# A two-layer S5 and gMLP trunk: the factors of B sent through DRAM on SyncE's queue, C's turn behind the first rows, both halves of two tables loaded at once, and the last sums of the scan on VectorE

## The chip, the core and the metric

One core of a Trainium2 chip runs the whole kernel. The metric is the device time of one execution in microseconds. Three runs of the kernel before gave 986.35, 982.47 and 985.27, a median of 985.27.

## The reference, cut

Two layers, each a stack of three post-normalised sub-layers on 256 tokens of width 1024: a SwiGLU feed-forward of width 2816, a mixer, and a second feed-forward. The mixer of the first layer is an S5 state-space model, that of the second a gMLP gate. The change touches the S5 mixer and its preparation alone:

```python
u = x @ w_in                                              # 256 x 1024, in 64 groups of 16 channels
lam = exp(a * dt)                                         # complex, 64 groups x 64 states
coef = (lam - 1) / a                                      # complex
bbar = coef[..., None] * b                                # complex, (group, state, channel)
bu = einsum('blgc,gpc->lbgp', u_groups, bbar)
h[t] = lam * h[t - 1] + bu[t]                             # scan over 256 tokens
y = Re(einsum('lbgp,gcp->blgc', h, c)) + d * u
y = gelu(y)
z = y * sigmoid(y @ w_glu + b_glu)
out = z @ w_out
```

## The kernel before, in words

Every product runs on TensorE in float32r with weights and activations split in two parts, `hi` and `lo`, and three matmuls for each product (`mm3`, `mm3t`). The weights are a single stream of blocks of 128 x 2048 (class `Stream`): SyncE loads a block into one of three `raw` buffers (line 63), ScalarE rounds it to `hi` (line 88 or 115), VectorE subtracts to get `lo` (line 89 or 119), and five pairs of split buffers are there. A load waits until the `lo` of the block that had its buffer is done, so SyncE's queue stands in the order of the program between loads and everything else that it issues. `tick` is called after every group of matmuls: it finishes the `lo` of the block before, issues the next load, rounds the next block, and calls one piece of background work.

The first feed-forward works through 11 chunks of 256 columns: four groups of 24 matmuls for the way in (lines 208 to 210, tile `ips`) and two groups of 12 for the way out of the chunk two before (lines 201 to 203, tile `acc`), six ticks in all.

Beside it runs the preparation of S5 (`prepare_s5`), as that background work: a list of steps, each with a first tick and a cost in us; a tick has 1.5 us of credit, and steps are taken from the list in order while credit is left. Steps of cost 0 are on other engines than VectorE. The ones that matter here:

- `coefs` and `coef` (lines 749 to 764): the discretisation factors of B, four complex sets, on VectorE.
- `spread` (769): writes these factors to DRAM and reads them back in another layout, 32 partitions at a time, five DMAs on GpSimd's queue. `load_b` and `c_load` (32 and 16 DMAs) and `seed` (small products for the tables) are on GpSimd too. The reads wait for the write to have landed.
- `c_turn` (905): VectorE transposes C, which `c_load` has brought; `b_rows` (844) multiplies B with the factors read back, and `b_turn` (853) transposes the result and sends it to DRAM as `rows`. `b_rows` and `b_turn` come eight times, `c_turn` ahead of the first.
- `table` (808) and `c_lam` (914): rotation tables and C times powers of lambda, both written to the DRAM tensor `tc`, half 0 and half 1 of its columns.

The mixer itself (`s5`) turns the scan over 256 tokens into eight tiles `ct` of 128 channels. For each: `inject` (TensorE, 16 matmuls `pps`), `forward` (a rotation on VectorE, `turned`, then two sums on GpSimd), `scan` (VectorE), `back` (rotation on VectorE, then two `sums` on GpSimd, into the one buffer `h`), `read_out` (TensorE, `yps`, which reads `h` and both halves of the table), `activate` (VectorE line 1118, then GELU on ScalarE), `split_y` (GpSimd), and `gate` (TensorE, `gacc`). The loop in lines 1225 to 1264 skews these over the tiles. Pieces of the weight split (`slow` rounds a block on ScalarE, `rest` does its `lo` in halves on VectorE, line 119) are placed in it. Behind the loop come eight `tanh` on ScalarE and eight `finish`, the gate's product on VectorE (lines 1159 to 1166), which TensorE needs tile by tile for the last product, `close_mixer`. Each engine works in the order of the program.

Of the kernel before, what the change touches and what calls it, by code (L numbers as in the profile page):

```python
# [27 lines left out]
CT = 8  # L28
T = 4
# [4 lines left out]
SUB = 2048  # L34
# [7 lines left out]
class Stream:  # L42
# [12 lines left out]
    def add(self, *parts):  # L55
        self.specs.append(parts)
        return len(self.specs) - 1
# [97 lines left out]
def hybrid(ctx: ExitStack, tc: tile.TileContext, a: dict, out: bass.AP, subs=SUBS):  # L155
    nc = tc.nc
# [19 lines left out]
    h = [const.tile([P, D], F32, name=f"h{t}") for t in range(2)]  # L176
# [35 lines left out]
    def load_ln(li, si, eng):  # L212
        g = ln_p.tile([P, D], F32, tag="gam", name="gam")
        b = ln_p.tile([P, D], F32, tag="bet", name="bet")
        eng.dma_start(out=g, in_=a["ln_g"][li, si:si + 1, :].broadcast_to([P, D]))
        eng.dma_start(out=b, in_=a["ln_b"][li, si:si + 1, :].broadcast_to([P, D]))
        return g, b
# [402 lines left out]
    def prepare_s5(sm, qp, dram):  # L620
# [9 lines left out]
        V, G, A = nc.vector, nc.gpsimd, nc.scalar  # L630
        MUL, ADD, SUB, MAX, MIN = ALU.mult, ALU.add, ALU.subtract, ALU.max, ALU.min
# [21 lines left out]
        val = {}  # L653
# [112 lines left out]
        def lam_power(d):  # L766
            cmul(val["lam"][d], val["lam"][d - 1], val["lam"][1])

        def spread():

            G.dma_start(out=res["cf"], in_=val["cfs"].rearrange("p t r j -> p t (r j)"))
            for t in range(T):
                G.dma_start(out=val["cqs"][32 * t:32 * t + 32].rearrange("p s r j -> p s (r j)"),
                            in_=res["cf"][:, t].rearrange("(s p) x -> p s x", p=32))
            A.copy(val["bf"], val["cf"][T - 1])

        def seed(i):

# [163 lines left out]
        def add(first, cost, f, *args):  # L942
            work.append((first, cost, lambda: f(*args)))
# [16 lines left out]
        add(5, 1.4, coefs)  # L960
        for t in reversed(range(T - 1)):
            add(5, 0.9, coef, t)
        add(5, 0, spread)
        for i in range(1, 7):
            add(5, 0, seed, i)
        for d in (2, 3):
            add(5, 0.9, lam_power, d)
            for n in (32, 64):
                add(5, 0, copy_b, d - 2, n)
        add(12, 1.6, c_turn)  # L970
        late = [(base_table, level) for level in range(4)]
        for part in range(4):
            for j in range(2):
                add(13, 1.9, b_rows, j, part)
                if part < 2:
                    add(10, 0, copy_b, part + 2, (32, 64)[j])
                add(10, 1.3, b_turn, j, part)
                if late:
                    add(10, 0, *late.pop(0))
        for j in range(2):  # L980
            add(10, 0, pads, j)
        for x in late:
# [31 lines left out]
    def s5(plan, res, qp, li, si, first, last):  # L1014
        cols, glu, rows = plan
        V, G = nc.vector, nc.gpsimd
# [8 lines left out]
        buf, pend = {}, []  # L1025
# [9 lines left out]
        def begin(c, t):  # L1035
            ps = acc_p.tile([P, 512], F32, tag="acc", name="ups")
            in_mm(cols[c], t, ps, range(4))
            return c, t, ps

        def end(c, t, ps):  # L1040
            in_mm(cols[c], t, ps, range(4, KD))
            ut = g_p.tile([P, 512], F32, tag="sgg", name="ut")
            nc.scalar.copy(ut, ps)
            V.transpose(uu[c][:, :, t], ps.rearrange("p (q c) -> p q c", c=32))
            pend.append((c, t, ut))
            if t == 1:
                done(cols[c])
# [13 lines left out]
        def load_tc(ct, half):  # L1061
            s = slice(512 * half, 512 * half + 512)
            nc.sync.dma_start(out=tcs[ct % 3][:, s], in_=res["tc"][ct, :, s])
# [16 lines left out]
            for j in range(2):  # L1080
                V.tensor_tensor(dst[j], src, tab[:, j].unsqueeze(1).broadcast_to([P, 2, 4, NS]), op=MUL)

        def sums(dst, src, ops):
            c, s = src
            for j in range(2):
                x, z = (c[:, 0], s[:, 1]) if j == 0 else (c[:, 1], s[:, 0])
                G.tensor_tensor(dst[:, j], x, z, op=ops[j])

        def scan(ct):
            f = fm[ct % 2].rearrange("p q k -> p (q k)")  # L1090
# [25 lines left out]
        def activate(ct):  # L1116
            yc = y[ct // 4][:, ct % 4]
            V.scalar_tensor_tensor(yc, in0=yc, scalar=res["d"][:, ct:ct + 1], in1=buf["yps"][ct % 2], op0=MUL, op1=ADD)
            nc.scalar.activation(yc, yc, AF.Gelu_apprx_tanh)
            nc.scalar.copy(yx(ct, 0), yc.rearrange("p (t k) -> p t k", t=2))  # L1120
# [34 lines left out]
        def finish(n):  # L1155

            x = half(n)
            z = buf["o"][n % 2][:, 0].rearrange("p q k -> p (q k)")
            V.scalar_tensor_tensor(z.rearrange("p (k t) -> p t k", t=T), in0=x.rearrange("p (t k) -> p t k", t=T), scalar=1.0,
                                   in1=y[n // 4][:, n % 4].rearrange("p (t k) -> p t k", t=T), op0=ADD, op1=MUL)  # L1160
            z = z.rearrange("p (t k) -> p t k", t=2)
            if n < 3:
                V.tensor_copy(yx(n, 0), z)
            else:
                nc.scalar.copy(yx(n, 0), z)
            V.tensor_tensor(yx(n, 1), z, yx(n, 0).bitcast(F32), op=SUB)
# [3 lines left out]
            turned(buf["p"], buf["pps"][ct % 2], ct)  # L1170
            sums(buf["v"][ct % 2], buf["p"], (ADD, SUB))

        def back(ct):
            turned(buf["o"], buf["s"], ct)
            sums(buf["h"], buf["o"], (SUB, ADD))

        later = []
        slow = lambda: later.extend(ws.split_slowly())
# [1 line left out]
        def rest(n):  # L1180
            for _ in range(min(n, len(later))):
                later.pop(0)()
# [3 lines left out]
            load_w(ct)  # L1186
        for ct in range(2):
            load_tc(ct, 0)
        end(*begin(0, 0))
        x = begin(1, 0)  # L1190
        make_xt(1, True)
# [24 lines left out]
        factors(1)  # L1216
        forward(1)
        end(*x)
        for ct in range(3):
            load_tc(ct, 1)  # L1220
        load_tc(3, 0)
        buffers()
        pieces = (0, 1, 1, 1, 1, 1, 1, 2, 2, 0)
# [1 line left out]
        for i in range(1, CT + 2):  # L1225
            if not later and pieces[i]:
                slow()
            if i - 1 < CT:
                read_out(i - 1)
                if i + 2 < CT:  # L1230
                    load_tc(i + 2, 1)
            if injected < CT:
                inject(injected)
                injected += 1
                if injected + 1 < CT:
                    load_w(injected + 1)
            if i == 1:
                turn_u()
                open_gate()
            if i == 2 and injected < CT:  # L1240
                inject(injected)
                injected += 1
                if injected + 1 < CT:
                    load_w(injected + 1)
            if 0 <= i - 2 < CT:
                gate(i - 2)
            if i + 1 < CT:
                factors(i + 1)
                if i > 2:
                    forward(i + 1)  # L1250
            if i < CT:
                scan(i)
                back(i)
                if i + 3 < CT:
                    load_tc(i + 3, 0)
            if i < 3:
                forward(i + 1)
            if i - 1 < CT:
                activate(i - 1)
                split_y(i - 1)  # L1260
            rest(pieces[i])
            if i == CT:
                slow()
                rest(2)
        ws.limit = None
        for n in range(CT):
            tanh(n)
        for n in range(CT):
            finish(n)
        gb = load_ln(li, si, nc.gpsimd)  # L1270
        close_mixer(rows, li, si, lambda k, t: (xth[t][:, k], xtl[t][:, k]), gb, 2 * ALPHA, 4 * EPS, last)

# [71 lines left out]
```

## Time and profile before

| what | value |
|---|---|
| median of three runs | 985.27 us (982.47 to 986.35) |
| the profiled execution, its own time | 983.81 us |
| its span, first to last instruction | 981.7 us |
| TensorE busy | 948.4 us, 97% of the span |
| VectorE, ScalarE, GpSimd busy | 650.1, 425.9, 165.6 us |
| mean granted TensorE clock | 0.990 |
| moved by DMA | 195.10 MB, 199 GB/s |

Lines of a view name the engine (PE is TensorE, PEld its weight loads, DVE VectorE, ACT ScalarE, POOL GpSimd, SP SyncE), the line of the program, and the tiles written and read. A busy TensorE includes ends that are modelled, since matmuls overlap; its idle time, and who ended it, is what the views show well. Times are from the start of the span.

### The profile page before, as it was taken

The numbers are of one execution on the slowest core, as the hardware profiler recorded it, in microseconds if no ns is written. First come the engines' busy times: TensorE is split into PE (matmuls) and PEld (weight loads), VectorE is DVE, ScalarE is ACT, GpSimd is POOL, SyncE is SP. The second block draws the span as 40 slices with busy tenths as digits, with TensorE's granted clock in tenths as the row PEclk, the third lists the DMA queues.
The fourth block names the chain that finished last, engine by engine and source line by source line (L and its number), as shares of the span: only waits on it lengthen the run. The fifth ranks groups of instructions, "written<-read, shape, count | busy, mean of one in ns | idle before, by whom it ended". The sixth has DMA issues, their size and how long they took to land.

```text
span 981.7 us, 16616 instructions
## 1 busy us (share of the span) xinstructions
PE 948.4 (97%) x6988; PEld 860.6 (88%) x6988; DVE 650.1 (66%) x801; ACT 425.9 (43%) x504; POOL 165.6 (17%) x249
## 2 busy tenths in 40 slices
PE   7997999999999999999999999999999999999996
PEld 5996989978887789999997999999879879999995
DVE  5858999778797955455467644536588766453635
ACT  5554355644335445343423634344345445433430
POOL 1868811001572100000002000000011010000001
PEclk9998999999899999999999999999999999999998
DMA  8874796968645665746466674655447457555521
GB/s 278 224 223 162 265 280 220 289 214 285 221 146 183 189 209 179 237 133 233 152 200 216 211 272 154 204 182 179 164 155 275 129 173 265 163 194 192 168 90 43
DMA packets 133354, 195.10 MB, mean 199 GB/s; under 512 B 7120, under 2 KB 103936, under 8 KB 133280
## 3 DMA queue, kind: packets, MB, share of 16 engines
q1 hardware_dynamic: 128432, 182.34, 56.0%
q0 software_dynamic: 4560, 11.19, 3.9%
q8 instruction: 54, 0.88, 0.4%
q10 hardware_dynamic: 288, 0.52, 0.1%
q14 instruction: 20, 0.16, 0.0%
HBM read 184.07 MB, written 9.96 MB: 198 GB/s over the span
## 4 chain that ended last, share of the span: by engine, by line
PE 66%; DVE 18%; DMA 6%; POOL 3%; issue 3%; ACT 2%; SPq 0%; POOLq 0%; DVEq 0%; ACTq 0%
PE ips L210 11%; PE ips L209 11%; PE ips L208 11%; PE acc L201 7%; PE acc L202 7%; PE acc L203 7%; DVE lo L89 4%; DVE lo L97 4%; PE pps L1075 2%; DVE pq L639 1%; PE ips L203 1%; DMA raw<-in_ffn_w_out 1%; DVE prod L639 1%; ACT hi L96 1%; PE ips L201 1%
## 5 line engine op out<-in xcount | busy, mean ns | idle before, releaser
L210 PE MATMUL ips<-xt,lo 128*128 128x256 f32 x1184 | 335.5, 283 | 2.8 <-DVE lo L89 2.2
L208 PE MATMUL ips<-xt,hi 128*128 128x256 f32 x1184 | 335.4, 283 | 0.0
L209 PE MATMUL ips<-xt,hi 128*128 128x256 f32 x1184 | 335.0, 283 | 0.0
L89 DVE TENSOR_TENSOR lo<-raw,hi 128x2048 fp32r<-128x2048 f32 x107 | 242.9, 2292 | 11.1 <-ACT hi L88 10.7
L210 PEld LDWEIGHTS ips<-xt,lo 128*128 128x128 f32 x1184 | 227.1, 192 | 3.6 <-DVE lo L89 2.8
L208 PEld LDWEIGHTS ips<-xt,hi 128*128 128x128 f32 x1184 | 227.1, 192 | 1.5
L209 PEld LDWEIGHTS ips<-xt,hi 128*128 128x128 f32 x1184 | 227.1, 192 | 1.4
L88 ACT CAST hi<-raw 128x2048 fp32r<-128x2048 f32 x107 | 204.1, 1909 | 47.2 <-PE acc L203 26.6
L202 PE MATMUL acc<-lo,gt 128*128 128x512 f32 x352 | 138.5, 393 | 6.6 <-DVE lo L89 6.6
L398 DVE TENSOR_TENSOR sgg<-ips,sgg 128x256 f32<-128x256 f32 x74 | 31.3, 423 | 163.9 <-ACT sgg L397 163.8
L201 PE MATMUL acc<-hi,gt 128*128 128x512 f32 x352 | 138.7, 394 | 0.6 <-ACT gt L406 0.5
L203 PE MATMUL acc<-hi,gt 128*128 128x512 f32 x352 | 137.8, 391 | 0.0
L397 ACT ACTIVATE sgg<-ips 128x256 f32<-128x256 f32 x74 | 28.3, 383 | 214.2 <-PE ips L210 213.0
L221 POOL TENSOR_SCALAR rstd<-mv 128x1 f32<-128x1 f32 x14 | 10.4, 741 | 636.8 <-DVE mv L247 613.0
L97 DVE TENSOR_TENSOR lo<-raw,hi 128x2048 fp32r<-128x2048 f32 (+2 forms) x52 | 89.6, 1754 | 22.6 <-ACT hi L96 22.4
L202 PEld LDWEIGHTS acc<-lo,gt 128*128 128x128 f32 x352 | 66.7, 189 | 20.0 <-DVE lo L89 7.5
L201 PEld LDWEIGHTS acc<-hi,gt 128*128 128x128 f32 x352 | 66.7, 189 | 14.2 <-ACT gt L406 1.3
L203 PEld LDWEIGHTS acc<-hi,gt 128*128 128x128 f32 x352 | 66.5, 189 | 14.3 <-DVE gt L407 0.3
L96 ACT CAST hi<-raw 128x2048 fp32r<-128x2048 f32 (+2 forms) x52 | 74.5, 1482 | 3.6 <-DMA raw<-in_ffn_w_in 2.9
L407 DVE TENSOR_TENSOR gt<-sgg,gt 128x256 fp32r<-128x256 f32 x74 | 31.3, 423 | 59.5 <-ACT gt L406 59.5
L406 ACT CAST gt<-sgg 128x256 fp32r<-128x256 f32 x74 | 30.1, 406 | 68.1 <-DVE sgg L398 67.9
L201 PE MATMUL ips<-hi,xt 128*128 128x512 f32 x112 | 44.9, 401 | 3.8 <-ACT xt L192 2.3
(230 smaller groups left out, 1227.0 us busy)
## 6 DMA issues: line engine op xcount, KB each, us to landing
raw<-in_ffn_w_in SPq DMA_DIRECT2D x172, 512.0 KB, 5.8
raw<-in_ffn_w_out SPq DMA_DIRECT2D x44, 1024.0 KB, 5.2
raw<-in_g_w_in SPq DMA_DIRECT2D x8, 1024.0 KB, 5.8
rows<-w SPq DMA_DIRECT2D x8, 512.0 KB, 3.8
raw<-in_s_w_in SPq DMA_DIRECT2D x4, 1024.0 KB, 7.2
raw<-in_s_w_glu SPq DMA_DIRECT2D x4, 1024.0 KB, 5.2
w<-rows SPq DMA_DIRECT2D x8, 512.0 KB, 5.3
tc<-tc SPq DMA_DIRECT2D x16, 256.0 KB, 5.4
```

Of the source, the lines that this page charges most:

```text
L88: nc.scalar.copy(hi, raw)
L89: self.unfinished.append(lambda: nc.vector.tensor_tensor(lo, raw, hi.bitcast(F32), op=ALU.subtract))
L96: nc.scalar.copy(hi[:, s], raw[:, s])
L97: eng[p % len(eng)].tensor_tensor(lo[:, s], raw[:, s], hi[:, s].bitcast(F32), op=ALU.subtract)
L201: nc.tensor.matmul(ps, xh, wh, start=start, stop=False)
L202: nc.tensor.matmul(ps, xh, wl, start=False, stop=False)
L203: nc.tensor.matmul(ps, xl, wh, start=False, stop=stop)
L208: nc.tensor.matmul(ps, wh, xh, start=start, stop=False)
L209: nc.tensor.matmul(ps, wh, xl, start=False, stop=False)
L210: nc.tensor.matmul(ps, wl, xh, start=False, stop=stop)
L398: nc.vector.tensor_tensor(g, ps[:, 1], sg, op=ALU.mult)
L407: nc.vector.tensor_tensor(x[:, 1], g, x[:, 0].bitcast(F32), op=ALU.subtract)
```

## The change

`spread` is split in two steps. The first writes the factors on SyncE's queue as soon as the last `coef` is done, and copies one set of them on ScalarE; the second, one tick later and behind one `lam_power`, reads them back with four DMAs on SyncE's queue. `c_turn` goes from ahead of the eight `b_rows` to behind the first two of them. In the mixer, half 1 of the tables 0 and 1 is loaded right after half 0 at the start of the stage, and no longer after the last part of the first product. In the last two iterations that have a scan (i = 6 and 7) the sums of `back` run on VectorE, with `activate` of the tile before between the rotation and the sums. The two last halves of the weight split go from the end of the loop to places behind the second and the fourth `finish`.

```diff
-        def spread():
-            G.dma_start(out=res["cf"], in_=val["cfs"].rearrange("p t r j -> p t (r j)"))
+        def spread(back):
+            if not back:
+                nc.sync.dma_start(out=res["cf"], in_=val["cfs"].rearrange("p t r j -> p t (r j)"))
+                A.copy(val["bf"], val["cf"][T - 1])
+                return
             for t in range(T):
-                G.dma_start(out=val["cqs"][32 * t:32 * t + 32].rearrange("p s r j -> p s (r j)"),
-                            in_=res["cf"][:, t].rearrange("(s p) x -> p s x", p=32))
-            A.copy(val["bf"], val["cf"][T - 1])
+                nc.sync.dma_start(out=val["cqs"][32 * t:32 * t + 32].rearrange("p s r j -> p s (r j)"),
+                                  in_=res["cf"][:, t].rearrange("(s p) x -> p s x", p=32))
...
-        add(5, 0, spread)
+        add(5, 0, spread, 0)
         for i in range(1, 7):
             add(5, 0, seed, i)
         for d in (2, 3):
             add(5, 0.9, lam_power, d)
             for n in (32, 64):
                 add(5, 0, copy_b, d - 2, n)
-        add(12, 1.6, c_turn)
+            if d == 2:
+                add(5, 0, spread, 1)
...
+            if part == 0:
+                add(12, 1.6, c_turn)
...
-        def sums(dst, src, ops):
+        def sums(dst, src, ops, eng=G):
...
-                G.tensor_tensor(dst[:, j], x, z, op=ops[j])
+                eng.tensor_tensor(dst[:, j], x, z, op=ops[j])
...
-        def back(ct):
+        def back(ct, between=None):
             turned(buf["o"], buf["s"], ct)
-            sums(buf["h"], buf["o"], (SUB, ADD))
+            if between:
+                between()
+            sums(buf["h"], buf["o"], (SUB, ADD), V if between else G)
...
         for ct in range(2):
             load_tc(ct, 0)
+        for ct in range(2):
+            load_tc(ct, 1)
...
-        for ct in range(3):
-            load_tc(ct, 1)
+        load_tc(2, 1)
         load_tc(3, 0)
...
-                back(i)
+                back(i, (lambda: activate(i - 1)) if i >= CT - 2 else None)
...
             if i - 1 < CT:
-                activate(i - 1)
+                if not CT - 2 <= i < CT:
+                    activate(i - 1)
                 split_y(i - 1)
             rest(pieces[i])
             if i == CT:
                 slow()
-                rest(2)
...
         for n in range(CT):
             finish(n)
+            if n in (1, 3):
+                rest(1)
```


## Rows read from the trace of the kernel before

**Rows 1.** What TensorE waited for over the whole span, by line: us in total, times, longest us (three of the thirteen rows).

```profile
PE acc L202 <- DVE lo L89: 6.6, 3, 5.8
...
PE yps L1113 <- DMA tc<-tc: 1.7, 1, 1.7
...
PE yps L1103 <- POOL rot L1087: 1.3, 2, 0.9
```

**Rows 2.** TensorE in order of time behind the long wait: start us, us, line, form, and in brackets the idle time before and its releaser. Nine matmuls start from 88.70 up to the one at 92.58, that one not counted.

```profile
88.70 0.80 PE L202 MATMUL acc<-lo,gt 128*128 128x512 f32 x1 [5.83 <-DVE lo L89]
...
92.58 0.39 PE L202 MATMUL acc<-lo,gt 128*128 128x512 f32 x1
92.81 0.39 PE L203 MATMUL acc<-hi,gt 128*128 128x512 f32 x1
```

**Rows 3.** Two stretches of 5 us: busy time of PE, PEld, DVE, ACT and POOL with their instructions, then granted clock, DMA share, GB/s.

```profile
85.00:90.00 5.00, 1.29 (x3) 1.10 (x4) 4.97 (x6) 3.85 (x4) 4.66 (x6) 0.56 0.29 94
...
250.00:255.00 5.00, 5.00 (x25) 4.90 (x23) 1.32 (x3) 0.47 (x1) 1.39 (x2) 0.50 0.30 75
```

**Rows 4.** TensorE in order of time in the S5 stage, columns as in Rows 2: the second half of the first read-out, the product behind it and the turn of u, and for comparison the first two of these lines again at 266 us.

```profile
249.15 0.88 PE L1113 MATMUL yps<-rot,tc 128*32 128x63 f32 x32 [1.75 <-DMA tc<-tc]
249.96 3.68 PE L1075 MATMUL pps<-uu,w 128*128 128x64 f32 x16
253.43 1.06 PE L1054 MATMUL tu<-ident,ut 128*128 128x128 f32 x4
...
266.13 0.62 PE L1113 MATMUL yps<-rot,tc 128*32 128x63 f32 x32
266.69 2.00 PE L1075 MATMUL pps<-uu,w 128*128 128x64 f32 x16
```

**Rows 5.** VectorE in order of time, 51 to 91 us: the last step of the factors of B, two weight halves, C's turn (two instructions), the first rows of B, and the two weight halves that TensorE waits for.

```profile
51.87 0.30 DVE L639 TENSOR_TENSOR fac<-p,q 128x32 f32<-128x32 f32 x2
...
56.20 4.49 DVE L89 TENSOR_TENSOR lo<-raw,hi 128x2048 fp32r<-128x2048 f32 x2
65.91 1.25 DVE L907 STREAM_TRANSPOSE cc<-cz 128x1024 f32<-128x1024 f32 x1 [5.23 <-DMA cz<-in_s_c_im]
67.19 0.43 DVE L645 TENSOR_SCALAR cc<-cc 128x512 f32<-128x512 f32 x1
...
75.88 1.42 DVE L639 TENSOR_TENSOR prod<-bq,fac 128x512 f32<-128x512 f32 x2 [6.06 <-DMA fac<-cf]
...
86.28 4.63 DVE L89 TENSOR_TENSOR lo<-raw,hi 128x2048 fp32r<-128x2048 f32 x2
```

**Rows 6.** GpSimd in order of time: the write of the factors to DRAM and the four reads back.

```profile
63.29 0.62 POOL L771 DMA_DIRECT2D cf<-fac  x1 [0.18 <-issue]
69.00 2.18 POOL L773 DMA_DIRECT2D fac<-cf  x4 [5.10 <-DMA cf<-fac]
```

**Rows 7.** SyncE's DMA issues in order of time, 46 to 62 us (start, length of the stretch of issues, line, transfer, how many).

```profile
46.58 4.30 SPq L63 DMA_DIRECT2D raw<-in_ffn_w_in  x4
58.55 0.37 SPq L63 DMA_DIRECT2D raw<-in_ffn_w_out  x1
60.72 10.05 SPq L63 DMA_DIRECT2D raw<-in_ffn_w_in  x4
```

**Rows 8.** Time from issue to landing of the factors' transfers: of the one write (line 771), and of the four reads (line 773).

```profile
DMA to landing us min/median/max: 5.4/5.4/5.4
...
DMA to landing us min/median/max: 2.0/3.5/5.2
```

**Rows 9.** A stretch of 2 us, columns as in Rows 3.

```profile
58.00:60.00 2.00, 2.00 (x19) 2.00 (x18) 2.00 (x2) 1.34 (x1) 1.74 (x4) 1.00 0.27 40
```

**Rows 10.** What TensorE waited for from 92 to 260 us, the two rows on the VectorE halves of the weight split.

```profile
PE acc L202 <- DVE lo L89: 0.8, 2, 0.5
PE ips L210 <- DVE lo L89: 0.7, 2, 0.4
```

**Rows 11.** Time from issue to landing of the weight loads that SyncE issued from 44 to 66 us.

```profile
DMA to landing us min/median/max: 4.7/6.3/8.2
```

**Rows 12.** VectorE in order of time in the S5 stage: the rotation that waits for the product of TensorE.

```profile
253.68 1.29 DVE L1081 TENSOR_TENSOR rot<-pps,tc 128x512 f32<-128x512 f32 x2 [3.87 <-PE pps L1075]
```

**Rows 13.** The page's DMA issues: size in KB and median us to landing of the same kind of weight load.

```profile
raw<-in_ffn_w_out SPq DMA_DIRECT2D x44, 1024.0 KB, 5.2
```

**Rows 14.** GpSimd in order of time: the two sums of `back` in iteration 6.

```profile
288.97 2.40 POOL L1087 TENSOR_TENSOR rot<-rot 128x256 f32<-128x256 f32 x2 [1.32 <-DVE rot L1081]
```

**Rows 15.** VectorE in order of time, the end of the S5 stage: D's term in iteration 6 (line 1118), four weight halves, and the first and the last instruction of the gate's eight products.

```profile
288.73 0.47 DVE L1118 SCALAR_TENSOR_TENSOR y<-y,dg,yps 128x256 f32<-128x256 f32 x1
...
299.39 5.17 DVE L119 TENSOR_TENSOR lo<-raw,hi 128x1024 fp32r<-128x1024 f32 x4
304.48 0.61 DVE L1159 SCALAR_TENSOR_TENSOR rot<-rot,y 128x256 f32<-128x256 f32 x1
...
315.36 0.42 DVE L1166 TENSOR_TENSOR xt<-rot,xt 128x256 fp32r<-128x256 f32 x1 [0.53 <-ACT xt L1165]
```

**Rows 16.** The page's groups: a VectorE instruction on two operands of 128 x 256.

```profile
L398 DVE TENSOR_TENSOR sgg<-ips,sgg 128x256 f32<-128x256 f32 x74 | 31.3, 423 | 163.9 <-ACT sgg L397 163.8
```

**Rows 17.** ScalarE in order of time: the eight tanh of the gate.

```profile
302.81 3.02 ACT L1153 ACTIVATE rot<-gacc,dg 128x256 f32<-128x256 f32 x8 [0.63 <-PE gacc L1145]
```

**Rows 18.** The chain that ended last, one of its pieces (start us, us, what): a weight load late in the first feed-forward.

```profile
184.39 11.98 DMA raw<-in_ffn_w_out
```

## The prediction

> **What bounds the kernel now.** TensorE is busy for nearly the whole span, so I read first what it waited for [rows 1]. Most of its waits are short; three belong to the lines of this change. The longest by far, 5.8 us, is for a weight half on VectorE in the first feed-forward. One of 1.7 us is for a table in the S5 stage, and two, 1.3 us together, are for the sums on GpSimd at the end of that stage. Second I read what stands behind such a wait. Behind the long one the matmuls start 0.43 us apart instead of 0.23: nine of them take 3.88 us (88.70 to 92.58) where nine at the later spacing take 2.07, so 1.81 us more are lost [rows 2]. The stretches show why: the granted clock is 0.56 in 85 to 90 us, and in the S5 stage 0.50 in 250 to 255 us, which is the lower level of 1.2 GHz, after TensorE had idled 5.83 and 1.75 us [rows 2, 3, 4]. In the S5 stage the 32 small matmuls behind the wait take 0.88 us against 0.62 at 266 us, and the 16 of the next product 3.68 against 2.00: 1.9 us more on these alone [rows 4]. So a wait costs more than its idle time, and two places, at 83 and at 248 us, cost 7.6 and at least 3.7 us.
>
> Third I asked why VectorE is late at 83 us. It idles twice before: 5.23 us ahead of C's turn, for a load of C, and 6.06 us ahead of the first rows of B, for the factors read back [rows 5]. The factors were done on VectorE at 52.2 us (51.87 and 0.30), but GpSimd, busy with its own program, issued their write at 63.29, and waited 5.10 us for it before the reads [rows 5, 6]. VectorE lost 11.3 us, TensorE felt 5.83 of them.
>
> **Part 1: factors on SyncE, C's turn later.** SyncE has issued four weight loads by 50.9 us, and its next is at 58.55 [rows 7], so the write can go out at 52.2. When does it land? On GpSimd's queue it took 5.4 us [rows 8], which gives 57.6. On SyncE's queue it stands behind the four loads, 2 MB; the DMA engines have run dry of them by 58 to 60 us, where their share is 0.27 [rows 9]. I take 59, the value nearer to the queue it will be in. The second step waits for that on SyncE, then issues four reads of 0.37 us, the price of an issue there [rows 7], until 60.5; reads took 2.0 to 5.2 us, median 3.5 [rows 8], so the last lands at 64.0. The Trainium skill, page "DMA: Bandwidth & Descriptors", section "Queues, rings and completion order", says that a ring takes its transfers in their order, which speaks against putting a small write behind big loads; by it the landing is at 59, without it at 57.6, and in both cases VectorE is free only at 63.0, so the sum hardly moves. No run so far shows the factors on that ring.
>
> VectorE comes out of two weight halves at 60.7 and has one more, 2.25 us (half of 4.49), so it is free at 63.0 and starts the first rows at 64.0 instead of 75.88: 11.9 us earlier [rows 5]. C's turn, 1.25 and 0.43 us, is still to be done, behind the first two rows, by when C has been there for long (it had landed at 65.9). At the next common point VectorE is 10.2 us ahead. The weight half that ended at about 88.6 would end near 78, and TensorE wants it at 82.9: 5 us to spare.
>
> TensorE can win the idle 5.83 and the clock's 1.81, 7.6 us, and, as VectorE then leads by 2.6 us more, the later waits on weight halves, 0.8 and 0.7 us [rows 10]: 9.1 at most. I take **8.5**, since not each of the later waits need go.
>
> What queues behind the new wait: SyncE's loads of 58.55 and 60.72, which go out at about 60.5 and 61, so 2.0 and 0.3 us late. The blocks they bring are the two whose halves stand at 86.28, and even 10 us earlier they are wanted at 76; landing takes at most 8.2 us [rows 5, 7, 11], so 7 us of cover remain. GpSimd loses five issues of 0.62 and 0.55 us and a wait of 5.10 [rows 6]; its seeds come earlier and nobody waits for them. C's turn pushes each later step of the preparation back by about one tick; the last two may not run before ticks 50 and 51 in any case. All three edits cost nothing beside this cover.
>
> Bounds: if both legs take the longest landing that SyncE's loads show, 8.2 us [rows 11], the rows start at 52.2 + 8.2 + 1.5 + 8.2 = 70.1 and the gain is 75.9 - 1.7 - 70.1 = 4.1. So 4.1 to 9.1.
>
> **Part 2: table halves at once.** The wait of 1.75 us goes, since half 1 is then loaded some 20 us before it is read. If the clock then stays up, the next product ends 1.75 + 0.26 + 1.68 = 3.7 us earlier, at 250.0 instead of 253.7, and the rotation on VectorE that waited 3.87 us for it starts that much earlier [rows 4, 12]. TensorE itself would win more (the turn of u and the opening of the gate ran on the low clock too, to 256), but the loop's end is set by the chain of VectorE and GpSimd, as its last read-outs show by waiting [rows 1]. I take **3.7**. What is late next: the second read-out, which needs sums on GpSimd that start only when the first has let go of the one buffer; it comes to within some tenths of TensorE.
>
> Bounds: with the clock down all the same, 1.75. The two transfers of 256 KB now stand ahead of weight loads at the start of the stage; the engines have room, and without it they cost half of what a 1024 KB load takes, 2.6 us [rows 13]. Above, 5.0, TensorE's own count. So -0.9 to 5.0.
>
> **Part 3: sums on VectorE, halves behind the gate's products.** In iteration 6 GpSimd ends the sums at 291.4 (288.97 and 2.40) [rows 14]. On VectorE they stand behind D's term, 288.73 + 0.47, and take two instructions of 0.42 [rows 15, 16]: 290.0. The two waits of TensorE, 1.3 us, go [rows 1]. VectorE pays 4 x 0.42 = 1.7 us. Then the gate: its first product waited for four weight halves until 304.48, though the first tanh was done at 303.2 (302.81 and an eighth of 3.02) [rows 15, 17]. With the waits gone and two halves moved away it starts at 301.9. But its eight products run 11.3 us (304.48 to 315.78), and two halves of 1.29 us now stand among them: 301.9 + 11.3 + 2.6 = 315.8, as before. TensorE starts its last product sooner and waits later, for the last tiles. I take **0.0**, between -1.3 (a gain, the two waits) and +1.7 (the four sums).
>
> **The sum.** 8.5 + 3.7 + 0.0 = 12.2 us off the profiled execution's 983.8: 971.6, say 971.5. That execution lies 1.5 us under the median of the runs shown and 1.3 over the lowest, which goes into the range.
>
> **The rivals.**
> 1. The clock falls in the S5 stage all the same, since the small matmuls remain. For: it fell after only 1.75 us of idling. Against: at 266 us the same lines run at full speed [rows 4]. 983.8 - 8.5 - 1.75 = 973.6. Chance 0.17.
> 2. The factors land late on the shared queue, both legs at 8.2 us. For: the four loads ahead. Against: the engines are nearly idle from 58 us [rows 9]. 983.8 - 4.1 - 3.7 = 976.0. Chance 0.10.
> 3. A transfer takes the gain back at the end of the feed-forward: the load issued at 184.39 needed 11.98 us where its kind needs 5.2 [rows 13, 18]. If that queue doesn't move, 6.8 of the 8.5 are lost: 983.8 - 1.7 - 3.7 = 978.4. Against: the load goes out when a VectorE half is done, and that moves. Chance 0.07.
> 4. The change doesn't bring the factors earlier: engines full of weight loads set their landing, and only issue time is saved, 0.62 + 4 x 0.55 - 5 x 0.37 = 1.0 us [rows 6, 7]: 983.8 - 1.0 - 3.7 = 979.1. Against: the 11 us before the write were GpSimd's program, not the transfer. Chance 0.06. The Trainium skill, page "DMA: Bandwidth & Descriptors", section "Issuing engines are not separate DMA queues", says just this, that another issuing engine saves issue time only; no run so far shows one transfer on both queues.
> 5. Slower: SyncE, held by the reads, starves VectorE of the factors for longer than GpSimd did. Break-even with part 2 needs rows at 77.9; slower by over 0.5% (4.9 us, about what a measurement here tells from no change) needs 82.8, so two landings of 14.6 us each. At 15.5 they start at 84.7: 983.8 + 10.5 - 3.7 = 990.6. The longest that the chain shows is 11.98 [rows 18]. Chance 0.03.
>
> **How the numbers follow.** The forecast has 0.57. The range takes the upper bounds of gain with the lowest run (983.8 - 9.1 - 5.0 - 1.3 - 1.3 = 967.1) to rival 2 with the median's 1.5 us and a little (978): 967 to 978, with 0.84 in it. Faster by over 0.5%: the forecast, rivals 1 and 2 and most of 3, 0.89; within: rival 4 and the rest of 3, 0.08; slower 0.03.
>
> **What would show it.** Part 1: no idle VectorE ahead of C's turn, first rows near 64, no TensorE wait at 83, clock 1.00 in 80 to 90 us. Part 2: no wait of line 1113 on `tc`, clock near 1.00 from 240 to 255. Part 3: 28 sums on GpSimd, four on VectorE, TensorE starting its last product earlier but waiting in it. I am wrong if the factors land after 70 us, if VectorE is late again before 185 us, or if the gate's last product ends later than the S5 gain.

## The result and the profile after

| | before | after |
|---|---|---|
| median of four runs each, on one chip | 985.41 us (982.47 to 986.35) | 972.03 us (970.98 to 972.36) |
| the profiled execution, its own time and span | 983.81, 981.7 us | 971.83, 969.7 us |
| mean granted TensorE clock | 0.990 | 0.998 |

The ratio is 0.9872, with a 95% interval of 0.9855 to 0.9890: the kernel is 1.3% faster. The forecast of 971.5 us is 0.5 us off. One run of the kernel before, in the third series of experiments below, took 1155.94 us at a granted clock of 0.755, a slower state of the chip, and is left out of all figures.

TensorE bounds both kernels, and its program is the same, so I compare when it starts each group of matmuls. The starts are from its order of time in the two profiled executions:

| TensorE starts | before | after | difference |
|---|---|---|---|
| the second group of the feed-forward (`tps`) | 28.79 | 30.39 | +1.60 |
| `acc`, ahead of the long wait | 82.38 | 83.78 | +1.40 |
| `ips`, behind it | 95.78 | 89.25 | -6.53 |
| `ips`, behind four short waits | 166.24 | 157.17 | -9.07 |
| `acc`, the last of the feed-forward | 213.54 | 204.80 | -8.74 |
| `tps`, behind its normalisation | 214.70 | 206.72 | -7.98 |
| `yps`, the first read-out of S5 | 245.83 | 237.85 | -7.98 |
| `yps`, the second read-out | 256.13 | 243.34 | -12.79 |
| `yps`, the seventh of the eight read-outs | 290.21 | 278.54 | -11.67 |
| `tps`, behind the last product of S5 | 327.36 | 315.14 | -12.22 |

The feed-forward gave 9.58 us (1.60 and 7.98), the S5 loop up to the seventh read-out 3.69, and what follows 0.55: 13.8 in all. The execution of after had lost 1.60 us in its first 29 us, ahead of all that was changed; so the two profiled spans differ by 12.0 only. The medians differ by 13.4. To add the 1.60 takes for granted that the kernel before would pass a late start on whole. In the profile of experiment 3, which has the old feed-forward, it did (1.50 us late at 29 us, 1.54 behind the long wait); in that of experiment 4 the wait took most of it in (3.43 late, then 0.81). So 13.8 is an upper figure.

First the waits of TensorE over the whole span, columns as in [rows 1]; three rows of ten.

```profile
PE ips L210 <- DVE lo L89: 2.2, 2, 1.5
PE acc L201 <- ACT xt L1170: 1.5, 3, 0.5
PE yps L1108 <- POOL rot L1092: 1.0, 1, 1.0
```

Of the three rows of [rows 1] the long wait and the wait for the table are gone, and on the sums of GpSimd there is one wait, in an earlier read-out, instead of two. The second row, in the last product of S5, stands where the kernel before had this one, on VectorE's tiles:

```profile
PE acc L201 <- DVE xt L1163: 1.0, 2, 0.7
```

Three stretches, columns as in [rows 3]; the product behind the first read-out of S5, at 249.96 us before [rows 4], starts at 239.80 now and falls into the middle one:

```profile
85.00:90.00 5.00, 5.00 (x27) 4.26 (x26) 4.49 (x8) 1.86 (x3) 4.09 (x13) 1.00 0.96 295
...
240.00:245.00 5.00, 5.00 (x99) 4.05 (x102) 4.96 (x7) 2.68 (x5) 3.00 (x4) 1.00 0.74 250
...
250.00:255.00 5.00, 5.00 (x115) 4.52 (x114) 3.68 (x6) 2.93 (x4) 4.23 (x5) 1.00 0.89 274
```

The granted clock is 1.00, the level of 2.4 GHz, in all three, where [rows 3] has 0.56 and 0.50. VectorE in order of time, the same steps as in [rows 5]:

```profile
53.74 0.29 DVE L639 TENSOR_TENSOR fac<-p,q 128x32 f32<-128x32 f32 x2
...
58.72 6.84 DVE L89 TENSOR_TENSOR lo<-raw,hi 128x2048 fp32r<-128x2048 f32 x3
65.49 1.35 DVE L639 TENSOR_TENSOR prod<-bq,fac 128x512 f32<-128x512 f32 x2
...
73.37 1.22 DVE L909 STREAM_TRANSPOSE cc<-cz 128x1024 f32<-128x1024 f32 x1
```

No bracket stands behind the first rows or C's turn: VectorE goes from its third weight half into the first rows at 65.49, and the factors have landed by then. SyncE's issues, as in [rows 7], and the landings of the factors, as in [rows 8]:

```profile
54.06 0.34 SPq L772 DMA_DIRECT2D cf<-fac  x1
59.78 3.00 SPq L776 DMA_DIRECT2D fac<-cf  x4
62.90 0.39 SPq L63 DMA_DIRECT2D raw<-in_ffn_w_out  x1
```

```profile
DMA to landing us min/median/max: 5.7/5.7/5.7
...
DMA to landing us min/median/max: 1.9/3.2/3.4
```

The write goes out as soon as the factors are done, and the reads go out 5.7 us later. The load at 62.90 has waited for them, and nobody waits for it. TensorE in the S5 stage, the lines of [rows 4]:

```profile
239.25 0.62 PE L1118 MATMUL yps<-rot,tc 128*32 128x63 f32 x32
239.80 2.00 PE L1080 MATMUL pps<-uu,w 128*128 128x64 f32 x16
...
260.04 0.32 PE L1108 MATMUL yps<-rot,cm 128*32 128x64 f32 x8 [0.96 <-POOL rot L1092]
```

The small matmuls take 0.62 and 2.00 us at their first use, where [rows 4] has 0.88 and 3.68. The last row is the new wait.

### The profile page after: what moved, and what is told of

Same layout as the page of the kernel before. It is cut to its first block, busy times and chain, and to the rows that moved or that the text cites. A ratio compares the mean times of both kernels' runs of the same rounds, so it can differ in the third digit from the quotient of the medians.

```text
span 969.7 us, 16611 instructions
## 1 busy us (share of the span) xinstructions
PE 944.7 (97%) x6988; PEld 857.9 (88%) x6988; DVE 650.9 (67%) x805; ACT 426.5 (44%) x504; POOL 162.8 (17%) x240
## 4 chain that ended last, share of the span: by engine, by line
PE 68%; DVE 8%; ACT 2%; issue 1%; POOL 1%; DMA 1%; POOLq 0%; DVEq 0%; ACTq 0%
PE ips L210 11%; PE ips L209 11%; PE ips L208 11%; PE acc L201 7%; PE acc L202 7%; PE acc L203 7%; DVE lo L97 3%; PE pps L1080 2%; PE ips L203 1%; ACT hi L96 1%; DVE lo L89 1%; DMA raw<-in_s_w_in 1%; PE ips L201 1%; PE ips L202 1%; PE zps L209 1%
## 5 line engine op out<-in xcount | busy, mean ns | idle before, releaser
L203 PEld LDWEIGHTS acc<-hi,gt 128*128 128x128 f32 x352 | 66.1, 188 | 14.3 <-DVE gt L407 0.2
L202 PEld LDWEIGHTS acc<-lo,gt 128*128 128x128 f32 x352 | 66.3, 188 | 12.2
```

The source lines that it names most:

```text
L202: nc.tensor.matmul(ps, xh, wl, start=False, stop=False)
L203: nc.tensor.matmul(ps, xl, wh, start=False, stop=stop)
```

## The experiments

Each kernel was timed beside the kernel before on one chip, which had medians of 984.31, 983.97 and 982.82 us in the three series (experiments 1 to 4, 5 to 8, 9 and 10). The line numbers shift with the edits.

**1. The factors on SyncE alone**; C's turn, tables and tail as before.

```diff
-            G.dma_start(out=res["cf"], in_=val["cfs"].rearrange("p t r j -> p t (r j)"))
+                nc.sync.dma_start(out=res["cf"], in_=val["cfs"].rearrange("p t r j -> p t (r j)"))
...
+            if d == 2:
+                add(5, 0, spread, 1)
```

> The kernel before with the factors of B on SyncE's queue alone; C's turn stays ahead of the first rows. Theory: the two idle times of VectorE stand one behind the other, so C's turn still waits for its load until about 66 us, then comes the one weight half, and the first rows start near 70 us instead of 75.9. The weight half that TensorE wants at 83 us is then ready just in time: the 5.8 us wait and the lower clock behind it go almost wholly, and the time falls by 5 to 7.6 us, to 978 to 980. Rival, each idle time is worth its own share of the stall: by 6.06/11.3 of 9.6, that is 5.1 us at most, and TensorE still waits about 2.7 us at 83 us. Rival, the gain is C's turn's: less than 2 us.

Measured: 974.93 us (972.71 to 976.32), ratio 0.9900 (0.9865 to 0.9935), a gain of 9.4 us, more than the 5 to 7.6 expected. VectorE, then TensorE, in order of time:

```profile
64.16 1.25 DVE L909 STREAM_TRANSPOSE cc<-cz 128x1024 f32<-128x1024 f32 x1 [2.02 <-DMA cz<-in_s_c_im]
...
68.00 1.43 DVE L639 TENSOR_TENSOR prod<-bq,fac 128x512 f32<-128x512 f32 x2
...
241.60 1.07 PE L1117 MATMUL yps<-rot,tc 128*32 128x63 f32 x32 [2.50 <-DMA tc<-tc]
```

C's turn stands where it stood, but its idle time is 2.02 us instead of 5.23 [rows 5], and VectorE is at the first rows at 68.00, 2 us sooner than I had expected, with C's turn done. TensorE starts the group at 95.78 us 6.49 us earlier, as in the changed kernel, and leaves the feed-forward 9.95 us ahead of its own start-up. So the whole of part 1 is the factors' way. About 1 us of it is lost again at the old wait for the table, which grows from 1.75 to 2.50 us.

**2. C's turn moved alone.**

```diff
-        add(12, 1.6, c_turn)
...
+            if part == 0:
+                add(12, 1.6, c_turn)
```

> The kernel before with C's turn behind the first two rows alone; the factors stay on GpSimd's queue. Theory: the first rows can't start before the factors land near 75.8 us, so nothing is gained, and C's 1.7 us of work now stand behind them instead of in front: 0 to 2 us slower, 985 to 987, with VectorE idle for about 13 us in one piece ahead of the first rows. Rival, each idle time is worth its share: 5.2/11.3 of 9.6, 4.4 us faster, 981.

Measured: 986.33 us (985.40 to 990.51), ratio 1.0028 (1.0009 to 1.0046), as expected. VectorE, then GpSimd, in order of time:

```profile
77.57 1.35 DVE L639 TENSOR_TENSOR prod<-bq,fac 128x512 f32<-128x512 f32 x2 [12.12 <-DMA fac<-cf]
...
63.38 2.18 POOL L639 TENSOR_TENSOR ch<-zq 128x32 f32<-128x32 f32 x1
...
67.69 0.62 POOL L771 DMA_DIRECT2D cf<-fac  x1 [0.18 <-issue]
73.91 2.19 POOL L773 DMA_DIRECT2D fac<-cf  x4 [5.60 <-DMA cf<-fac]
```

The two idle times of [rows 5] became one of 12.12 us: the factors set the end, and what VectorE does in the meantime counts for nothing. The write went out at 67.69 instead of 63.29, behind small GpSimd instructions, and that is part of the 2 us by which this kernel is slower; whether the move brought it about, no run shows.

**3. The table halves alone.**

```diff
+        for ct in range(2):
+            load_tc(ct, 1)
...
-        for ct in range(3):
-            load_tc(ct, 1)
+        load_tc(2, 1)
```

> The kernel before with both halves of tables 0 and 1 loaded at once, alone. Theory: the wait of 1.75 us on line 1113 goes, the granted clock stays at its upper level from 240 to 260 us, and the rotation that waited for the product comes 3.7 us earlier: 3.7 us faster, up to 4.9, that is 980.5 to 981.7. Rival, the clock falls all the same: 1.75 us faster, 983.7.

Measured: 980.28 us (979.08 to 981.78), ratio 0.9956 (0.9939 to 0.9973), a gain of 4.0 us, as expected. A stretch, as in [rows 3], and one wait of TensorE:

```profile
250.00:255.00 5.00, 5.00 (x110) 3.96 (x109) 5.00 (x7) 2.80 (x5) 3.54 (x4) 1.00 0.64 221
...
PE yps L1103 <- POOL rot L1087: 2.2, 3, 1.0
```

The granted clock stays at 1.00 without the wait for the table, though the small matmuls remain. TensorE wins 4.82 us from the first read-out to the second (+1.48 to -3.34) and gives 1.13 back in a new wait on GpSimd's sums, in the fourth read-out: 3.69 net.

**4. The tail alone** (sums of iterations 6 and 7 on VectorE, the two weight halves behind products of the gate).

```diff
-            sums(buf["h"], buf["o"], (SUB, ADD))
+            sums(buf["h"], buf["o"], (SUB, ADD), V if between else G)
...
-                rest(2)
...
+            if n in (1, 3):
+                rest(1)
```

> The kernel before with the sums of iterations 6 and 7 on VectorE and the two weight halves behind the second and fourth of the gate's products, alone. Theory: TensorE's two waits on GpSimd go, the gate starts up to 2.5 us sooner, but its last tile comes only 0.5 us sooner, since the halves stand among the products: 0 to 1 us faster, 984.4 to 985.4, no difference that a measurement shows. Rival, the two waits are won whole: 1.3 us or more. Rival, VectorE is full and pays for the sums: 1.7 us slower.

Measured: 982.61 us (981.64 to 985.81), ratio 0.9989 (0.9970 to 1.0008): no difference by the timing, as expected. In the trace TensorE is 0.67 us ahead at the seventh read-out, 3.20 at the start of the last product and 1.21 behind it, a net 0.54, as in the changed kernel (0.55). The lead is given back while the product waits for the gate's tiles, 1.5 us in three waits on ScalarE.

**5. The changed kernel again.** No edit.

> The changed kernel again, unaltered, beside the three others of this series: 971 to 973 us, 12 to 13.5 us under the kernel before. It gives the spread against which the others are read; TensorE's start-up, which took 0.2 to 3.4 us longer than in the first profile in the five profiles so far, should differ here too by one or two us.

Measured: 972.64 us (970.97 to 973.90), ratio 0.9873 (0.9836 to 0.9910), as expected. In its trace the start is 3.13 us later than in the kernel before, and the feed-forward gives 10.6 us, counted as above (3.13 and 7.49).

**6. The changed kernel, C's turn back in its old place.**

```diff
+        add(12, 1.6, c_turn)
...
-            if part == 0:
-                add(12, 1.6, c_turn)
```

> The changed kernel with C's turn back ahead of the first rows; all else stays. Theory since the first series: with the factors off GpSimd's queue C has landed by 64 us, VectorE waits about 2 us for it, the first rows start 2.5 to 3 us later than in the changed kernel, and the weight half that TensorE wants is still ready some 2 us early. So the order of C's turn is worth nothing by itself: within 1 us of the changed kernel. Rival, as the prediction counted it: each us by which the rows start later is a us of VectorE's lead lost, and TensorE pays for it later in the feed-forward: 2 to 3 us slower than the changed kernel.

Measured: 972.63 us (971.04 to 973.13), ratio 0.9872 (0.9841 to 0.9902). VectorE in order of time:

```profile
63.60 1.25 DVE L909 STREAM_TRANSPOSE cc<-cz 128x1024 f32<-128x1024 f32 x1 [1.06 <-DMA cz<-in_s_c_im]
...
67.49 1.35 DVE L639 TENSOR_TENSOR prod<-bq,fac 128x512 f32<-128x512 f32 x2
```

An idle microsecond on VectorE, and no wait of TensorE from 82 to 150 us. The move of C's turn is worth nothing here, as expected.

**7. The factors on GpSimd's queue, but early**: write and reads on GpSimd, ahead of the loads of C and the seeds.

```diff
-        for j in range(2):
-            add(2, 0, c_load, j)
...
-                nc.sync.dma_start(out=res["cf"], in_=val["cfs"].rearrange("p t r j -> p t (r j)"))
+                G.dma_start(out=res["cf"], in_=val["cfs"].rearrange("p t r j -> p t (r j)"))
...
                 add(5, 0, spread, 1)
+                for j in range(2):
+                    add(5, 0, c_load, j)
+                for i in range(1, 7):
+                    add(5, 0, seed, i)
```

> The changed kernel with the factors' five transfers on GpSimd's queue again, but early in its program: the loads of C and the seeds stand behind them instead of in front. Theory, the place in the queue counts and not the engine: the write goes out at about 54 us as on SyncE, the rows start within 2 us of the changed kernel, and the time is within 1.5 us of it (C lands near 75 us, and its turn may wait for it about 1 us). Rival, SyncE's queue is itself the gain: the rows start 3 us or more later than in the changed kernel, and the time is 2 to 6 us worse.

Measured: 975.47 us (974.12 to 976.92), ratio 0.9903 (0.9872 to 0.9934): 2.8 us worse than the changed kernel, where I had expected it within 1.5. GpSimd, then VectorE, in order of time:

```profile
55.38 0.62 POOL L772 DMA_DIRECT2D cf<-fac  x1 [0.45 <-DVE fac L639]
59.59 0.56 POOL L776 DMA_DIRECT2D fac<-cf  x1 [3.59 <-DMA cf<-fac]
...
66.24 1.29 DVE L639 TENSOR_TENSOR prod<-bq,fac 128x512 f32<-128x512 f32 x2
...
78.39 1.25 DVE L909 STREAM_TRANSPOSE cc<-cz 128x1024 f32<-128x1024 f32 x1 [4.61 <-DMA cz<-in_s_c_im]
```

The first rows start at 66.24, as early as with SyncE. So for the first rows it is the place in a queue that counts, and not the engine: in the kernel before GpSimd's program kept the write from being issued for 11 us (52.17 to 63.29 [rows 5, 6]). The Trainium skill, page "DMA: Bandwidth & Descriptors", section "Issuing engines are not separate DMA queues", says that DMAs issued by SyncE, ScalarE and GpSimd run on the same 16 DMA engines, and that issuing from several of them saves issue time alone. The trace agrees roughly as far as the landing goes: the write took 3.9 us here and 5.7 on SyncE's queue in the changed kernel. But the loads of C and the seeds now stand behind, and VectorE idles 4.61 us for C. I take the lost 3 us as the price of that; no run parts C from the seeds.

**8. More on VectorE**: sums of iteration 2 too, and all eight casts of the gate's product instead of three.

```diff
-                back(i, (lambda: activate(i - 1)) if i >= CT - 2 else None)
+                back(i, (lambda: activate(i - 1)) if i >= CT - 2 or i == 2 else None)
...
-            if n < 3:
+            if n < 9:
```

> The changed kernel with the sums of iteration 2 on VectorE too, as those of 6 and 7, and all eight casts of the gate's products on VectorE instead of five of them on ScalarE. Theory: the wait of 1.0 us that TensorE has for GpSimd's sums at 259 us goes, and the gate's products take 0.14 us less each where VectorE waited for the cast: 0.5 to 1.8 us faster than the changed kernel. Rival, the loop is bound by VectorE and the two more sums cost it 0.7 us: no gain in the loop, 0 to 0.7 us from the casts alone.

Measured: 971.26 us (970.21 to 975.65), ratio 0.9869 (0.9832 to 0.9906), which can't be told from the changed kernel. The wait that the sums were moved for did not go: it is 1.35 us in the fourth read-out, where the changed kernel has 0.96. That read-out needs the sums of iteration 3, which stayed on GpSimd, so the edit took the wrong iteration. In the trace the sums lose 0.6 us (TensorE's lead falls from 12.62 to 10.90 us over the loop, where it falls from 12.79 to 11.67 in the changed kernel), and the casts win: 1.90 us from the seventh read-out to the end of the last product, instead of 0.55.

**9. The casts alone** (`n < 9` in the changed kernel).

> The changed kernel with all eight casts of the gate's product on VectorE instead of three (five left ScalarE). Theory, from the run with more on VectorE: TensorE gives back 1.15 us in the tail by waiting for casts on ScalarE, and without these waits the tail gains about 1.3 us, so about 970.7 beside the changed kernel's 972.0. Rival: the casts on VectorE take as long as the waits that they remove, since VectorE must do eight products alone, and the time stays at 972 within 0.5 us. If it is the extra sums on VectorE that paid in that run, this one stays at 972.0 too.

Measured: 971.31 us (969.50 to 974.22), ratio 0.9884 (0.9858 to 0.9910). From the seventh read-out to the end of the last product TensorE wins 1.91 us instead of 0.55, the size that was expected, but not by the way that was expected. The three waits in the product stay, 1.3 us in all, now on VectorE's tiles, where they were 1.5 us on ScalarE's. What goes is the wait of 0.78 us behind the product, for VectorE's normalisation. By the timing the gain isn't shown, since 971.31 lies closer to the changed kernel's medians, 972.03 and 972.64, than the runs scatter. I take the 1.4 us as shown in the traces of two kernels only. One more wait of this profile, ahead of the S5 stage, matters below; TensorE in order of time and a stretch:

```profile
206.31 1.69 PE L187 MATMUL tps<-ident,h 128*128 128x128 f32 x8 [2.32 <-DVE h L231]
...
208.00:210.00 2.00, 2.00 (x6) 1.52 (x6) 1.34 (x3) 1.97 (x2) 0.00 (x0) 0.50 0.00 0
```

**10. The write of the factors on ScalarE's queue**, the reads on SyncE's.

```diff
-                nc.sync.dma_start(out=res["cf"], in_=val["cfs"].rearrange("p t r j -> p t (r j)"))
+                A.dma_start(out=res["cf"], in_=val["cfs"].rearrange("p t r j -> p t (r j)"))
```

> The changed kernel with the write of the factors on ScalarE's queue, on which no weight load stands, and the reads on SyncE's as before. By the order of a queue (the write stands behind the weight loads that SyncE issued just before) the landing falls from 5.2 to 6.0 us on SyncE's queue to about 4.2, as on GpSimd's queue in the run that had it early. By the rival, that it is the engines' load at that moment and not the queue, it stays at 5.2 to 6.0. The time does not change in either case, since the first rows start when VectorE comes out of a weight half: 972 within 1.5 us.

Measured: 974.86 us (974.17 to 976.65), ratio 0.9922 (0.9892 to 0.9952). The landing of the write, ScalarE, VectorE and TensorE in order of time:

```profile
DMA to landing us min/median/max: 6.0/6.0/6.0
...
55.31 0.24 ACT L773 COPY ch<-fac 128x64 f32<-128x64 f32 x1 [4.43 <-DVE fac L639]
...
69.55 1.51 DVE L639 TENSOR_TENSOR prod<-bq,fac 128x512 f32<-128x512 f32 x2
...
162.79 0.38 PE L210 MATMUL ips<-xt,lo 128*128 128x256 f32 x1 [1.09 <-DVE lo L89]
```

On the time I was wrong: no change was expected, and it is 2 to 3 us worse than the changed kernel (972.03 and 972.64); beside the kernel before in its own series it wins 8.0 us, where those won 13.4 and 11.3. ScalarE's queue waited 4.43 us for the factors, the rounding of weights queued behind it came late, and VectorE came to the first rows at 69.55 instead of 65.49. The long wait of TensorE is gone here too (+2.40 to -5.53 against the kernel before, 7.93 us), but three short waits on weight halves stand behind it where the changed kernel has one, and the feed-forward gives 7.8 us instead of 9.6. On the landing the rival's figure came out: 6.0 us on a queue with no weight load ahead. The Trainium skill, page "DMA: Bandwidth & Descriptors", section "Queues, rings and completion order", says that each DMA engine takes the transfers of one ring in their order; no run here shows that order in the write's landing, which took 5.2 to 5.9 us on SyncE's queue, 6.0 on ScalarE's, and 3.9 to 5.9 on GpSimd's.

## Why the prediction was right, step by step

**The factors' way (part 1), 8.5 predicted, 9.6 measured.** The mechanism was right. VectorE had the factors 1.87 us later than in the kernel before (53.74 and 51.87); with that taken off, the write went out at 52.2 (predicted 52.2), the reads at 57.9 (59), and the first rows at 63.6 (64.0). One step on the way was wrong and cost nothing: I had VectorE free at 63.0 and waiting for the last factors until 64.0, while it came out of its third weight half at 63.7, with the factors landed, and did not wait. That the time of the first rows agrees so well is partly luck. The stall and the low clock gave 7.93 us (+1.40 to -6.53), where 7.64 was predicted. What was mis-sized is the term of the later waits: "9.1 at most", with 1.5 us for four waits, priced at their idle time. They gave 2.54 (-6.53 to -9.07). One of them, TensorE of the kernel before in order of time, and the one new wait of the kernel after:

```profile
131.82 0.28 PE L209 MATMUL ips<-xt,hi 128*128 128x256 f32 x1
132.53 0.39 PE L210 MATMUL ips<-xt,lo 128*128 128x256 f32 x1 [0.43 <-DVE lo L89]
```

```profile
158.72 0.28 PE L209 MATMUL ips<-xt,hi 128*128 128x256 f32 x1
159.74 0.39 PE L210 MATMUL ips<-xt,lo 128*128 128x256 f32 x1 [0.74 <-DVE lo L89]
```

Between two such matmuls 0.12 us is usual. The first wait holds the next start back by 0.71, so it costs 0.59 before its successors pay a little more, and the lead changed by 0.69 there, for an idle time of 0.43. All four together: 1.49 us idle, 2.54 lost. The new one: 0.74 idle, 0.99 lost. A short wait costs about a quarter of a microsecond beyond its idle time, and I had seen that only for the long one. With 2.54 the upper bound would have been 10.2. Of my signs of being wrong, "VectorE is late again before 185 us" came true in this one wait of 0.74 us. The 9.6 itself is one profile's: to the same mark, and counted the same way, the traces of experiments 5, 8 and 9, with the same feed-forward, give 10.6, 9.9 and 9.8.

**C's turn.** I let the gain rest on its move ("no idle VectorE ahead of C's turn"), and experiments 1 and 6 show that it bears nothing: with C's turn ahead of the first rows, VectorE starts it at 64.16 and 63.60 us and waits only 2.02 and 1.06 us for C. I had taken C's landing of 65.9 from the trace of before as fixed. It differs from run to run: C's last load landed between 62.1 and 67.1 us in the four profiles that send the factors late on GpSimd's queue, and between 61.9 and 64.2 in the seven that send them early and load C in the old place. So I can't say that the factors' move brought C earlier. Alone, the move of C's turn doesn't help (experiment 2). That a gain remains for a case where C lands later is possible; no run shows it.

**The queue behind the new wait.** SyncE's next load went out at 62.90 instead of 58.55, 2.8 us later beside the start-up, where I had 2.0, and cost nothing, as predicted.

**The tables (part 2), 3.7 predicted, 3.69 measured**, in the changed kernel and alone. That TensorE's own 4.8 would not all be kept, because a read-out then waits for sums on GpSimd, was right. But I had named the second read-out, which starts at 243.34 without a wait; the row at 260.04 is the fourth, and its 0.96 us idle cost 1.10 (-12.78 to -11.68). So the agreement is in part luck: what makes 3.7 of the 4.8 was lost two read-outs later than I had it.

**The tail (part 3), 0.0 predicted, 0.55 measured**, inside its bounds. That the lead would be spent in waiting for the last tiles was right; what of it the sums and what the halves give was not taken apart.

**The rivals.** The clock in S5 stayed up (1, refuted by experiment 3: the small matmuls alone, without the wait, did not bring it down). The factors landed in 5.7 and at most 3.4 us, not 8.2 (2). A transfer took some of the gain back at the end of the feed-forward (3), though another one than I had named, as shown below. The write had been held by GpSimd's program and not by the engines (4, experiment 7). SyncE starved nobody (5).

**The end of the feed-forward.** TensorE is 9.07 us ahead at 157 us and 7.98 at 207. Of the 1.09 between, 0.99 went at the one new wait; then 0.66 more were won, and 0.76 lost at `tps`, which waits for the normalisation on VectorE. TensorE there, before and after, then the chain and ScalarE after:

```profile
214.70 1.23 PE L187 MATMUL tps<-ident,h 128*128 128x128 f32 x8 [0.78 <-DVE h L231]
```

```profile
206.72 1.23 PE L187 MATMUL tps<-ident,h 128*128 128x128 f32 x8 [1.53 <-DVE h L231]
...
186.43 10.33 DMA raw<-in_s_w_in
...
196.78 1.91 ACT L96 CAST hi<-raw 128x2048 fp32r<-128x2048 f32 x1 [1.02 <-DMA raw<-in_s_w_in]
```

VectorE's last weight half stands ahead of the normalisation, ScalarE rounds that block, and the block's load took 10.33 us. So rival 3 held in a small part: 0.76 of its 6.8 us. Among the seven other profiles with the factors early the same wait was 0.77 to 0.94 us in five, 1.79 in experiment 10, and 2.32 in experiment 9, whose granted clock was 0.50 behind it (208 to 210 us) and which lost 3.1 us of its lead there. This place is the next to look at.

**The sum.** 12.2 were predicted and up to 13.8 measured where the change acts, of which the start of this execution hid 1.6; so the profiled time agrees with the forecast more closely than its terms do. That the forecast is only 0.5 off the median is luck in part too: it was counted from an execution 1.6 us under the median of before, and the gain by the medians is 1.2 larger than the 12.2. By the medians the gain is 13.4, and its interval, 10.8 to 14.3 us, holds both.

## What to carry to other kernels

When an engine waits for a transfer, look first at when the transfer was issued and what its issuer was doing until then: here 11 of the 17 us from the factors done to their write landed were the issuer's program. A queue that is free at that moment is worth having only if nothing urgent stands behind the wait on it; SyncE had 7 us of cover by the prediction's count, and ScalarE and the front of GpSimd's list had none. Price a wait of TensorE by the start of the next group and not by its idle time, which was too small at each of the six waits that I worked out in the first feed-forward.

## What the runs showed of the hardware

The start of an execution differs by some microseconds from run to run, ahead of any change: the group at 28.79 us started between 0.2 and 3.4 us later in the eleven other profiles. TensorE in order of time, in the kernel after:

```profile
13.19 0.63 PE L203 MATMUL ips<-hi,xt 128*128 128x512 f32 x1
13.61 0.63 PE L201 MATMUL ips<-hi,xt 128*128 128x512 f32 x1
...
17.16 0.39 PE L201 MATMUL ips<-hi,xt 128*128 128x512 f32 x1
```

Up to 16.6 us the matmuls start 0.43 us apart, and then 0.23; in the kernel before they are 0.23 apart from 12.2 us on. The granted clock is given as 1.00 in 12 to 18 us of both, so I can't say from it what held them back.

The length of an idle time alone did not tell whether the clock fell behind it. The granted clock fell to the lower level of 1.2 GHz, or had it for a part of the stretch, behind idle times of 5.83 and 1.75 us in the kernel before (0.56 and 0.50 [rows 3]), of 2.50 in experiment 1 (0.60 in 241 to 244 us) and of 2.32 in experiment 9 (0.50). It stayed at 1.00 behind 1.78 us in experiment 2 (128 to 132 us), 1.71 in experiment 7 (120 to 124) and 1.79 in experiment 10 (209 to 213), and behind the 0.96 and 1.53 of the changed kernel. What made the difference between 1.75 and 1.79 no run here shows.

Small GpSimd instructions that began beside a weight half of VectorE ended with it: in experiment 2 the one at 63.38 took 2.18 us, to 65.56, and VectorE's two weight halves ran from 60.86 to 65.44; in the kernel before the same instruction took 0.25 us, at 60.92, when VectorE idled. GpSimd's write of the factors, which stands behind these instructions in four profiles, went out between 63.29 and 68.83 us in them; SyncE's went out between 53.57 and 55.22 in six. I take these instructions and the start-up as the reason of the wider spread; no run parts the two.
